# A decoder layer on one core: an early conditioning load moved up the load queue, one chunk's matmuls put in passes, and one weight split moved into the last softmax

## The chip, the core and the metric

The kernel runs on one core of one Trainium2 chip. The metric is the device time of one execution in microseconds (us): 1576.35 us is the median of three runs of the kernel before. Engines are named as in the profile: PE is TensorE's matmul row and PEld its weight-load row, DVE is VectorE, ACT is ScalarE, POOL is GpSimd, SP is SyncE, whose queue (SPq) issues nearly all loads. Instructions of one engine run in the order in which they are written; an instruction that has to wait holds back all that stand behind it on its engine.

## The reference

One layer of a decoder trunk over 512 tokens of width 2048, in float32, cut to what the change touches:

```python
c_act = jax.nn.silu(c)
mod = c_act @ w_ada[l] + b_ada[l]                  # 2048 -> 3 * 2048
shift, scale, gate = jnp.split(mod, 3, axis=-1)
h = rmsnorm(x, attn_norm_g[l]) * (1.0 + scale[:, None]) + shift[:, None]
proj = h @ w_in[l]                                 # q_lat, kv_lat, k_rope, z, u, v, z, g, g
...
p = jax.nn.softmax(s, axis=-1)                     # 16 heads, causal
...
merged = jax.nn.sigmoid(g_mla) * y_mla + jax.nn.sigmoid(g_sgu) * y_sgu
x = x + gate[:, None] * (merged @ w_out[l])
return rmsnorm(x, final_norm_g)
```

## The kernel before

**Products.** Every float32 operand of a large product is split in two: a rounded high part (ACT, a cast) and the remainder (DVE, a subtraction). A product is then three matmuls that add up in one PSUM bank: high by high, high by low, low by high. The helper `mm3` (lines 147 to 149) issues these three one behind the other. One matmul takes a 128x128 block of weights and a 128x512 moving operand.

**Weights as a stream.** The weights come in granules of up to 1024 columns, in one fixed order. `Stream` keeps that order: `dma_to(i)` issues loads up to granule `i` into three raw buffers (`wraw0` to `wraw2`), and `split_to(i)` splits granules up to `i` into two pairs of buffers (`w0h`/`w0l`, `w1h`/`w1l`): the cast is line 117, the subtraction line 118. A granule that is already split is not split again, for the loop begins at the first one that is not:

```python
    def split_to(self, i):
        i = min(i, len(self.src) - 1)
        while self.n_split <= i:
            ...
            self.nc.scalar.copy(hi[:, :n], raw[:, :n])
            self.nc.vector.tensor_tensor(out=lo[:, :n], in0=raw[:, :n], in1=hi[:, :n].bitcast(F32), op=ALU.subtract)
```

`get(i, ahead)` splits up to granule `i + ahead`, then issues loads three granules further. `load_before(granule, f)` hangs another load in front of a granule's own load on the same queue.

**The first stage.** The layer's input is multiplied chunk by chunk: 16 chunks of 128 input channels, each with the x tile `xt[j]` (256 KB, the `X` tiles), the first-stage granule `g1[j]` (512 KB, `wraw<-in_w`) and the adaLN scale chunk `KC + j` (KC is 16; 1 MB, `wada<-in_wada`). `ada_load` (line 356) loads an adaLN chunk and `ada_dot` reduces it on DVE against `silu(c)` (line 138, `wada<-wada,cact`). From that comes `gxA` (line 144), the factor of this chunk's 128 channels; ACT scales the x tile to the high part `hh[j]` (line 425), DVE makes the low part `hl[j]` (line 138). Eight banks `ps1[0]` to `ps1[7]` gather 1024 output columns, so that a chunk is 24 matmuls. For the first chunk they run pass by pass (line 434): all eight banks with the high parts, then all eight with the weights' low part, then all eight with `hl`. For the others they run bank by bank through `mm3`.

The order on DVE within a chunk is: dot, `gxA`, low part of the granule, `hl`, and the sum of squares of the chunk before (line 135, `cosT<-cosT,XS`). On ACT it is: cast of the granule, `hh`, square of the x tile. The four `wada` buffers first hold the small tiles from which `silu(c)` is spread over the partitions (`crow`, `csplit`, `pick`) and chunk 16; chunk 17 takes the buffer of `crow`, chunk 18 that of `csplit`, and so on, each once the old tile is free.

**The end of attention.** Heads 0 to 15 run one after the other: scores, softmax, projections of the next head, transposes of the softmax, product with v, gates. In `softmax` DVE masks and takes maxima, ACT exponentiates the four row blocks in two pairs (line 1559), and between the pairs a caller's function may run (`between`, which splits a granule). DVE then divides by the sums (lines 1547 and 142). The last head (15) has no next head; in the place of its projections stand the first two granules of the output projection, `go[0, 0]` and `go[0, 1]` (two times 24 matmuls over four banks), by `out_granule`. Behind them come the transposes of head 15's softmax (line 1577).

For head 15 the function that runs between the two pairs is `split_to(go[0, 0])`. That granule is next in the stream behind the last key granule, and `kproj(15)`, by `get` with one granule ahead, has split it by then.

Of the kernel before, what the change touches and what calls it, by code (L numbers as in the profile page):

```python
# [23 lines left out]
KC = D // P  # L24
NB = S // P
H = 16
# [101 lines left out]
def trunk_layer(ctx, tc, xT, xn, c, vecs, pos, wada, w1, w2, wv, wv3, wv4, wh, wh15, wq, wqr, wk, wvv, wo, wsT, bsp, gfin, out,  # L128
                dbg=None):
    nc = tc.nc  # L130
    ACT, DVE, PE, DMA = nc.scalar, nc.vector, nc.tensor, nc.sync
    LEFT, RIGHT = "left", "right"

    def tt(out, in0, in1, op):
        DVE.tensor_tensor(out=out, in0=in0, in1=in1, op=op)  # L135

    def stt(out, in0, scalar, in1, op0, op1, **kw):
        DVE.scalar_tensor_tensor(out=out, in0=in0, scalar=scalar, in1=in1, op0=op0, op1=op1, **kw)  # L138

    def ts(out, in0, s1, s2, op0, op1=None):  # L140
        if op1 is None:
            DVE.tensor_scalar(out=out, in0=in0, scalar1=s1, scalar2=None, op0=op0)
        else:
            DVE.tensor_scalar(out=out, in0=in0, scalar1=s1, scalar2=s2, op0=op0, op1=op1)

    def mm3(ps, ah, al, bh, bl, start, stop):
        PE.matmul(ps, ah, bh, start=start, stop=False)  # L147
        PE.matmul(ps, ah, bl, start=False, stop=False)  # L148
        PE.matmul(ps, al, bh, start=False, stop=stop)  # L149
# [18 lines left out]
    def nt(p, shape, dt, tag, **kw):  # L168
        uid[0] += 1
        return p.tile(shape, dt, tag=tag, name=f"{tag}_{uid[0]}", **kw)  # L170
# [11 lines left out]
    ws = Stream(nc, [(wp, f"wraw{i}") for i in range(3)], [(wp, f"w{i}") for i in range(2)])  # L182
# [79 lines left out]
    g1 = [ws.add(w1[k], GW) for k in range(KC)]  # L262
    z14 = lambda k, n: wh[H - 2, 0, k // 8][:, k % 8 * P:(k % 8 + n) * P]
    g2 = [ws.add([(0, S, w2[k][:, :S]), (S, P, z14(k, 1))], 640) for k in range(KC)]
    gq, gr, gk, gvv = {}, {}, {}, {}
# [35 lines left out]
    go = {}  # L301
# [9 lines left out]
    def get(i, ahead=1, run=1):  # L311
        r = ws.get(i, ahead)
        fs, pend[:] = pend[:run], pend[run:]
        for f in fs:
            f()
        return r
# [11 lines left out]
    def bank():  # L328
        n_bank[0] += 1
        return bank_at(ring[(n_bank[0] - 1) % len(ring)])  # L330
# [28 lines left out]
    def ada_dot(j):  # L359
        t = ada_tiles.pop(j)  # L360
        if j == KC:
            for q, sl in enumerate(quarters):
                stt(t[:, sl], t[:, sl], 1.0, cps[q], ALU.mult, ALU.mult, accum_out=dot0[:, q:q + 1])
            DVE.tensor_reduce(out=dots[:, j:j + 1], in_=dot0, axis=AX.X, op=ALU.add)
            ts(b1, vec[:, C_BADA + KC:C_BADA + 2 * KC], 1.0, None, ALU.add)
        else:
            stt(t, t, 1.0, cact, ALU.mult, ALU.mult, accum_out=dots[:, j:j + 1])

    def load_before(granule, f, *a):
        ws.before.setdefault(granule, []).append(lambda: f(*a))  # L370
# [3 lines left out]
    DMA.dma_start(vec, vecs)  # L374
    for j in range(KC):
        if j > 0:
            load_before(g1[max(j, 2)], ada_load, KC + j)
            load_before(g1[j], lambda j: DMA.dma_start(xt[j], xT[j]), j)
        load_before(SHIFT_AT[j], ada_load, j)
    load_before(g2[0], lambda: DMA.dma_start(cact_d, cact[0:1]))  # L380

    hh, hl = [None] * KC, [None] * KC
    ssx = cosT

    def square_of(j):
        if j == 0:
            ACT.activation(ssx, xt[j], AF.Square)
            return None
        sq = sqw[:, j % 2]
        ACT.activation(sq, xt[j], AF.Square)  # L390
        return sq
# [23 lines left out]
    ps1 = [bank() for _ in range(8)]  # L415
    sq = None
    for j in range(KC):
        if j > 0:
            ada_dot(KC + j)
        A = gxA[:, j:j + 1]  # L420
        ts(A, dots[:, KC + j:KC + j + 1], b1[:, j:j + 1], vec[:, C_GX + j:C_GX + j + 1], ALU.add, ALU.mult)
        wH, wL = get(g1[j], ahead=0)
        hh[j] = nt(hp.p, [P, S], F32R, f"hh{j}")
        hl[j] = nt(hp.p, [P, S], F32R, f"hl{j}")
        ACT.activation(hh[j], xt[j], AF.Copy, scale=A)  # L425
        stt(hl[j], xt[j], A, hh[j].bitcast(F32), ALU.mult, ALU.subtract)
        if sq is not None:
            tt(ssx, ssx, sq, ALU.add)
        sq = square_of(j)
        cols = [slice(m * P, (m + 1) * P) for m in range(8)]  # L430
        if j == 0:
            for a, b in ((wH, hh[j]), (wL, hh[j]), (wH, hl[j])):
                for m in range(8):
                    PE.matmul(ps1[m], a[:, cols[m]], b, start=(a is wH and b is hh[j]), stop=False)
        else:
            for m in range(8):
                mm3(ps1[m], wH[:, cols[m]], wL[:, cols[m]], hh[j], hl[j], False, j == KC - 1)
# [57 lines left out]
    for j in range(KC):  # L495
        fix_begin(j)
        wH, wL = get(g2[j])
# [136 lines left out]
    for st in range(KC):  # L634
# [5 lines left out]
        wH, wL = get(gb[st], ahead=0 if st == KC - 1 else 1)  # L640
# [63 lines left out]
    def place(s, us, f, *a):  # L704

        def full(s):
            own, (a, b) = busy.get(s, 0.0) + us, (busy.get(s + d, 0.0) for d in (-1, 1))
            return own > 3.3 or own + max(a, b) > 5.75

        while full(s):  # L710
            s += 1
        spend(s, us)
        on(s, BACK, f, *a)
        return s
# [240 lines left out]
    for g in range(H):  # L955
# [3 lines left out]
        a = s_ + 4  # L959
        on(a, BACK, sgu_scale)  # L960
        a = place(a, 0.29, sgu_weights)
        a = place(a, 0.29, sgu_weights_split)
        if g + 1 < H:
            on(a + 1, LOAD, sgu_load, g + 1)
        a = place(max(a, s_ + 5), 0.69, sgu_gain)
        a = place(a + 1, 0.69, sgu_split)
# [369 lines left out]
    for b in range(len(BLOCKS)):  # L1336
        if b == 1:
            ring[:], n_bank[0] = [5, 6], 0
        for g, (p, i) in enumerate(V7):
# [17 lines left out]
            if i == 0 and p in (1, 5, 6):  # L1357
# [3 lines left out]
            wH, wL = (w.rearrange("p (k h w) -> p k h w" if BLOCKS[b][0] == "v" else "p (h k w) -> p k h w", h=4, k=2)  # L1361
                      for w in vparts.pop((b, g)))
# [108 lines left out]
    def rproj(p):  # L1471
        wH, wL = get(gr[p])
        ps = bank_at(0)
        for k in range(6):
            sl = slice(k * P, (k + 1) * P)
            mm3(ps, wH[:, sl], wL[:, sl], lh[k], ll[k], k == 0, k == 5)
        return ps
# [47 lines left out]
    def scores(h):  # L1525
        qh, ql = qt.pop(h)
        kh, kl = kt.pop(h)
        q2 = qs.pop(h)
        s3, s2, s1 = bank(), bank(), bank()
        dst = {3: s3, 2: s2[:, :384], 1: s1[:, :256], 0: s1[:, 256:384]}  # L1530
        for i in (3, 2, 1, 0):
            ps = dst[i]
            n = (i + 1) * P
            q = slice(i * P, (i + 1) * P)
            mm3(ps, qh[:, q], ql[:, q], kh[:, :n], kl[:, :n], True, False)

            PE.matmul(ps, q2[:, q], krh[:, :n], start=False, stop=False)  # L1537
            PE.matmul(ps, q2[:, q], krl[:, :n], start=False, stop=True)  # L1538
        return dst
# [78 lines left out]
    def merge(n=None):  # L1618
        fs, merging[:] = merging[:n], merging[n:] if n else []
        for f in fs:  # L1620
            f()
# [22 lines left out]
    for h in range(H):  # L1644
        if h == H - 1:
            ring[:], n_bank[0] = [4, 5, 6, 7], 0
        dst = scores(h)
        more, odd = h + 1 < H, h % 2 == 1
        pair = h // 2 + 1
        first = go[0, 0] if not more else gr[pair] if not odd and 2 * pair < H else None  # L1650
        pr_, shares_ = softmax(h, dst, (lambda: ws.split_to(first)) if first is not None else None)
        if more:
            qproj(h + 1, lambda: merge(1 if h == H - 2 else None))
            if not odd and 2 * pair < H:
                rps = rproj(pair)
        else:
            pso = [bank_at(k) for k in range(NB)]
            for i in range(2):
                out_granule(0, i, pso)
        pa, fa = transposes(pr_, (0,))  # L1660
        fa()
        if h < GATED:
            for n in range(NB):
                g_ = gt[h][:, n * P:(n + 1) * P]
                ACT.activation(g_, g_, AF.Copy, scale=shares_[:, n:n + 1])
        pb, fb = transposes(pr_, (1,))
        fb()
        pc, fc = transposes(pr_, (2, 3))
        fc()
        if more:  # L1670
            kps = kproj(h + 1)
            kfinish(h + 1, kps)
        else:
            merge()
            pieces_at(h)
            DVE.tensor_reduce(out=dots[:, 2 * KC:2 * KC + NG], in_=partial, axis=AX.X, op=ALU.add)
            gate_sum(0, NG)
            out_granule(0, 2, pso)
            gate_turn(0, NG, bank(), nt(tp, [P, S], F32, "sig", bufs=3))()
        gate_ = gt[h]  # L1680
        if h < GATED:
            gate_ = nt(tp, [P, S], F32, "sig", bufs=3)
            ACT.copy(gate_, turn(gt[h]))
        tps = turn(vt[h])
        ops = pv(h, {**pa, **pb, **pc})
        merge_a(h, ops, tps, gate_)
        if not odd:
            pieces_at(h)
        if not odd and 2 * pair < H:
            m2 = at("m2", F32)  # L1690
            swapped(m2, rps)
        if more and odd:
            rfinish(pair, rps, m2)
            vproj(pair)
# [92 lines left out]
    for n in range(NB):  # L1787
        tk = slice(n * P, (n + 1) * P)

        for part, (o, w) in enumerate(((0, S),) if n < NB - 1 else ((0, half), (half, half))):  # L1790
            last = o + w == S
            ps = bank()[:, :w]
            for j in range(H):
                sl = slice((j % 2) * 512 + o, (j % 2) * 512 + o + w)
                wH, wL = wl[j // 2]
# [91 lines left out]
```

## Time and profile before

| what | us |
|---|---|
| three runs | 1574.80, 1576.35, 1576.39 |
| median of the three | 1576.35 |
| the profiled execution, its own time | 1576.21 |
| its span, from the first to the last instruction | 1574.5 |
| PE busy within the span | 1558.1 |
| DVE busy | 1221.5 |
| ACT busy | 801.4 |
| mean granted TensorE clock | 0.997 |

The page gives for each engine its busy time; the timeline gives single instructions with their start, their length and, in brackets, how long the engine sat idle before and what released it; the view by windows gives for a stretch of time each engine's busy time with the number of instructions, the granted clock (1.00 is full) and what the DMA engines moved. All times are counted from the span's start. Matmuls overlap in the records: the distance from one start to the next is what a matmul costs, and it is shorter than the length shown.

### The profile page before, as it was taken

How to read it: one execution, taken by the hardware profiler on the slowest of the kernel's cores; microseconds unless marked ns; L12 is line 12 of the kernel's file. 1: busy time of each engine (PE TensorE's matmuls, PEld its weight loads, DVE VectorE, ACT ScalarE, POOL GpSimd, SP SyncE). 2: the span in 40 equal slices, each digit the busy share in tenths (PEclk: the TensorE clock that was granted, in tenths of full speed). 3: DMA queues.
4: the chain of work that ended last, by engine and by line, in shares of the span. 5: the costliest groups of instructions: out<-in, count | busy, mean ns of one | idle time of the engine just before them, and what ended most of it. 6: DMA issues, size and time to landing. Idle time of an engine off the chain costs nothing. (4 is left out here: it accounts for less than half of the span.)

```text
span 1574.5 us, 20617 instructions
## 1 busy us (share of the span) xinstructions
PE 1558.1 (99%) x7400; PEld 1297.6 (82%) x7400; DVE 1221.5 (78%) x1665; ACT 801.4 (51%) x1238; POOL 70.3 (4%) x67
## 2 busy tenths in 40 slices
PE   9999999999999999999999999999999999999998
PEld 7888778888888888888888888887888888888886
DVE  7989777778787879787879697968777777865753
ACT  4344555546554546455546464647655566532332
POOL 0000000100010000010100010100000000000000
PEclk9999999999999999999999999999999999999999
DMA  9979565859786877787767785966433333338722
GB/s 380 357 265 341 180 182 169 237 140 266 232 231 173 230 210 213 208 220 202 206 169 205 207 246 157 261 172 211 148 118 119 127 116 117 98 127 331 263 88 107
DMA packets 237224, 316.16 MB, mean 201 GB/s; under 512 B 16201, under 2 KB 184193, under 8 KB 231489
## 3 DMA queue, kind: packets, MB, share of 16 engines
q1 hardware_dynamic: 214066, 291.25, 55.9%
q0 software_dynamic: 22912, 23.07, 9.6%
q8 instruction: 58, 0.95, 0.3%
q10 hardware_dynamic: 144, 0.52, 0.1%
q14 instruction: 44, 0.36, 0.1%
HBM read 291.11 MB, written 23.68 MB: 200 GB/s over the span
## 5 line engine op out<-in xcount | busy, mean ns | idle before, releaser
L135 DVE TENSOR_TENSOR X<-X,X 128x1024 fp32r<-128x1024 f32 (+2 forms) x110 | 129.4, 1182 | 29.7 <-ACT X L620 26.8
L620 ACT CAST w0h<-X 128x1024 fp32r<-128x1024 f32 x70 | 73.6, 1052 | 95.0 <-PE ps L1369 56.5
L620 ACT CAST X<-X 128x1024 fp32r<-128x1024 f32 x69 | 72.5, 1051 | 89.8 <-PE ps L1369 52.4
L620 ACT CAST w1h<-X 128x1024 fp32r<-128x1024 f32 x70 | 73.6, 1051 | 82.5 <-PE ps L1369 44.4
L135 DVE TENSOR_TENSOR w0l<-X,w0h 128x1024 fp32r<-128x1024 f32 x70 | 85.6, 1222 | 27.1 <-ACT w0h L620 26.8
L135 DVE TENSOR_TENSOR w1l<-X,w1h 128x1024 fp32r<-128x1024 f32 x70 | 85.5, 1222 | 26.0 <-ACT w1h L620 24.3
L147 PE MATMUL ps<-hh,w1h 128*128 128x512 f32 (+1 forms) x260 | 103.9, 400 | 1.6 <-ACT hh L425 1.4
L148 PE MATMUL ps<-hl,w1h 128*128 128x512 f32 (+1 forms) x260 | 102.3, 393 | 0.5 <-DVE hl L138 0.5
L149 PE MATMUL ps<-hh,w1l 128*128 128x512 f32 (+1 forms) x260 | 102.2, 393 | 0.0
L118 DVE TENSOR_TENSOR w0l<-wraw,w0h 128x1024 fp32r<-128x1024 f32 (+4 forms) x61 | 64.3, 1053 | 42.0 <-ACT w0h L117 40.3
L135 DVE TENSOR_TENSOR X<-wraw,X 128x1024 f32<-128x1024 f32 (+1 forms) x66 | 80.6, 1221 | 19.5 <-ACT X L620 17.0
L117 ACT CAST w0h<-wraw 128x1024 fp32r<-128x1024 f32 (+4 forms) x61 | 56.0, 918 | 75.0 <-issue 22.0
L1370 PE MATMUL ps<-w1l,hh 128*128 128x512 f32 x236 | 92.3, 391 | 1.7 <-DVE w1l L135 1.7
L147 PE MATMUL ps<-hh,w0h 128*128 128x512 f32 x238 | 93.7, 394 | 0.0
L117 ACT CAST w1h<-wraw 128x1024 fp32r<-128x1024 f32 (+4 forms) x60 | 50.5, 841 | 83.2 <-issue 23.9
L148 PE MATMUL ps<-hl,w0h 128*128 128x512 f32 x238 | 92.8, 390 | 0.0
L149 PE MATMUL ps<-hh,w0l 128*128 128x512 f32 x238 | 92.7, 389 | 0.0
L1370 PE MATMUL ps<-w0l,hh 128*128 128x512 f32 x236 | 92.2, 391 | 0.4 <-DVE w0l L135 0.4
L1368 PE MATMUL ps<-w1h,hh 128*128 128x512 f32 x236 | 92.0, 390 | 0.2 <-ACT w0h L620 0.2
L1368 PE MATMUL ps<-w0h,hh 128*128 128x512 f32 x236 | 92.0, 390 | 0.0
L1369 PE MATMUL ps<-w1h,hl 128*128 128x512 f32 x236 | 91.9, 389 | 0.0
L1369 PE MATMUL ps<-w0h,hl 128*128 128x512 f32 x236 | 91.9, 389 | 0.0
(398 smaller groups left out, 4380.9 us busy)
## 6 DMA issues: line engine op xcount, KB each, us to landing
X<-in_wh SPq DMA_DIRECT2D x131, 512.0 KB, 4.9
wada<-in_wada SPq DMA_DIRECT2D x39, 1024.0 KB, 7.0
wraw<-in_wo SPq DMA_DIRECT2D x32, 512.0 KB, 4.4
wraw<-in_wh SPq DMA_DIRECT2D x21, 512.0 KB, 5.4
wraw<-in_wh POOLq DMA_DIRECT2D x21, 512.0 KB, 7.7
X<-in_wv SPq DMA_DIRECT2D x17, 512.0 KB, 3.5
X<-in_wh SPq DMA_DIRECT2D x22, 384.0 KB, 3.5
half<-in_w SPq DMA_DIRECT2D x32, 256.0 KB, 4.3
```

The source lines that it names most:

```text
L117: self.nc.scalar.copy(hi[:, :n], raw[:, :n])
L118: self.nc.vector.tensor_tensor(out=lo[:, :n], in0=raw[:, :n], in1=hi[:, :n].bitcast(F32), op=ALU.subtract)
L135: DVE.tensor_tensor(out=out, in0=in0, in1=in1, op=op)
L147: PE.matmul(ps, ah, bh, start=start, stop=False)
L148: PE.matmul(ps, ah, bl, start=False, stop=False)
L149: PE.matmul(ps, al, bh, start=False, stop=stop)
L620: ACT.copy(hi, t)
L1368: PE.matmul(ps[t].rearrange("p (h w) -> p h w", h=4), xh[:, tk], wH[:, k], start=st, stop=False, skip_group_check=True)
L1369: PE.matmul(ps[t].rearrange("p (h w) -> p h w", h=4), xl[:, tk], wH[:, k], start=False, stop=False, skip_group_check=True)
L1370: PE.matmul(ps[t].rearrange("p (h w) -> p h w", h=4), xh[:, tk], wL[:, k], start=False, stop=sp, skip_group_check=True)
```

## The change

```diff
     DMA.dma_start(vec, vecs)
     for j in range(KC):
         if j > 0:
-            load_before(g1[max(j, 2)], ada_load, KC + j)
+            load_before(g1[j], ada_load, KC + j)
             load_before(g1[j], lambda j: DMA.dma_start(xt[j], xT[j]), j)
         load_before(SHIFT_AT[j], ada_load, j)
...
-        if j == 0:
+        if j <= 1:
             for a, b in ((wH, hh[j]), (wL, hh[j]), (wH, hl[j])):
                 for m in range(8):
-                    PE.matmul(ps1[m], a[:, cols[m]], b, start=(a is wH and b is hh[j]), stop=False)
+                    PE.matmul(ps1[m], a[:, cols[m]], b, start=(j == 0 and a is wH and b is hh[j]), stop=False)
         else:
             for m in range(8):
                 mm3(ps1[m], wH[:, cols[m]], wL[:, cols[m]], hh[j], hl[j], False, j == KC - 1)
...
     for h in range(H):
         if h == H - 1:
             ring[:], n_bank[0] = [4, 5, 6, 7], 0
+            ws.split_to(go[0, 0])
         dst = scores(h)
         more, odd = h + 1 < H, h % 2 == 1
         pair = h // 2 + 1
-        first = go[0, 0] if not more else gr[pair] if not odd and 2 * pair < H else None
+        first = go[0, 1] if not more else gr[pair] if not odd and 2 * pair < H else None
         pr_, shares_ = softmax(h, dst, (lambda: ws.split_to(first)) if first is not None else None)
```

No instruction is added or taken away on any engine: PE, DVE, ACT, POOL and SP have as many as before. The order moves at three places.

On SP, at the program's start, in the order of issue (`wada_194` is adaLN chunk 17 after the change, `wada_197` the same chunk before; `wada_199` is chunk 18; `X_35` is the tile that holds x chunks 0 and 1, `wraw_1` granule `g1[1]`):

```order
 L374 DMA vec_88<-in_vecs 128x92
+L356 DMA wada_194<-in_wada 128x2048
 L378 DMA X_35_179<-in_xT 128x512
-L98 DMA wraw_1_195<-in_w 128x1024
-L356 DMA wada_197<-in_wada 128x2048
+L98 DMA wraw_1_197<-in_w 128x1024
 L356 DMA wada_199<-in_wada 128x2048
 L378 DMA X_36_180<-in_xT 128x512
```

Chunk 17 stood behind x chunk 1 and granule 1, and now stands ahead of both; chunk 18 and all that follows keep their places.

On PE, in the first stage's second chunk (`hh_65` and `hl_66` are `hh[1]` and `hl[1]`, `w1h_367` and `w1l_368` the two parts of granule 1, `ps_53` to `ps_60` the eight banks), before:

```order
L434 MATMUL ps_60_325<-hl_63_337,w0h_327 128x512
L147 MATMUL ps_53_318<-hh_65_376,w1h_367 128x512
L148 MATMUL ps_53_318<-hl_66_377,w1h_367 128x512
L149 MATMUL ps_53_318<-hh_65_376,w1l_368 128x512
L147 MATMUL ps_54_319<-hh_65_376,w1h_367 128x512
L148 MATMUL ps_54_319<-hl_66_377,w1h_367 128x512
```

and after, at the end of the first of its three passes:

```order
L434 MATMUL ps_58_323<-hh_65_376,w1h_367 128x512
L434 MATMUL ps_59_324<-hh_65_376,w1h_367 128x512
L434 MATMUL ps_60_325<-hh_65_376,w1h_367 128x512
L434 MATMUL ps_53_318<-hh_65_376,w1l_368 128x512
L434 MATMUL ps_54_319<-hh_65_376,w1l_368 128x512
```

The 24 matmuls are the same; `hl[1]` was read by the second of them and is now read by the seventeenth, `w1l` by the third and now by the ninth.

On DVE, in the softmax of head 15 (`d_1395` and `hl_1833` hold its exponentials, `mx` its maxima and sums, `wraw_97` is granule `go[0, 1]`, `wraw_98` granule `go[0, 2]`):

```order
 L142 TENSOR_SCALAR d_1395_9078<-d_1395_9078,mx_12144 128x512
 L142 TENSOR_SCALAR d_1395_9078<-d_1395_9078,mx_12144 128x384
+L118 TENSOR_TENSOR w0l_12162<-wraw_97_11920,w0h_12161 128x1024
 L1547 RECIPROCAL mx_12144<-mx_12144 128x2
 L142 TENSOR_SCALAR hl_1833_12145<-hl_1833_12145,mx_12144 128x256
 L142 TENSOR_SCALAR hl_1833_12145<-hl_1833_12145,mx_12144 128x128
-L118 TENSOR_TENSOR w0l_12171<-wraw_97_11920,w0h_12170 128x1024
 L118 TENSOR_TENSOR w1l_12201<-wraw_98_12021,w1h_12200 128x1024
```

and on ACT at the same place:

```order
 L1559 ACTIVATE d_1395_9078,mx_12144<-ps_1829_12121,mx_12144 128x512
 L1559 ACTIVATE d_1395_9078,mx_12144<-ps_1830_12122,mx_12144 128x384
+L117 CAST w0h_12161<-wraw_97_11920 128x1024
 L1559 ACTIVATE hl_1833_12145,mx_12144<-ps_1831_12123,mx_12144 128x256
 L1559 ACTIVATE hl_1833_12145,mx_12144<-ps_1831_12123,mx_12144 128x128
-L117 CAST w0h_12170<-wraw_97_11920 128x1024
 L117 CAST w1h_12200<-wraw_98_12021 128x1024
```

The granule that moves is `go[0, 1]`, the output projection's second: both halves of its split stood behind the softmax and now stand between its two pairs. The new call `ws.split_to(go[0, 0])` ahead of the scores issues nothing, since that granule is split already.

## The prediction

> **What bounds the kernel now.** I read the page's busy times first, then the waits of PE, then the two places of the change in the timeline. PE is busy for nearly the whole span, and the view of waits (time in all, times, longest) shows the few stretches in which it is held up:
>
> ```profile
> PE 1558.1 (99%) x7400; PEld 1297.6 (82%) x7400; DVE 1221.5 (78%) x1665; ACT 801.4 (51%) x1238; POOL 70.3 (4%) x67
> PE ps L147 <- ACT hh L425: 1.4, 1, 1.4
> PE ps L148 <- DVE w0l L118: 0.8, 1, 0.8
> PE ps L148 <- DVE hl L138: 0.5, 1, 0.5
> ```
>
> So a microsecond counts only where PE waits or runs slowly, and these three waits lie at the change's places. The view by windows adds what the waits don't show (columns: length; PE, PEld, DVE, ACT and POOL busy; granted clock, DMA share, GB/s):
>
> ```profile
> 11.08:16.90 5.82, 5.73 (x24) 4.42 (x24) 3.15 (x3) 1.41 (x2) 0.48 (x1) 1.00 1.02 412
> 16.90:18.20 1.30, 0.01 (x1) 0.01 (x1) 1.26 (x4) 0.78 (x2) 0.00 (x0) 1.00 1.04 429
> 20.10:23.50 3.40, 3.40 (x10) 2.65 (x9) 3.36 (x6) 1.35 (x3) 0.00 (x0) 0.52 1.03 418
> 80.00:100.00 20.00, 20.00 (x90) 16.57 (x89) 16.66 (x21) 9.26 (x14) 0.00 (x0) 1.00 0.65 210
> ```
>
> PE is idle from 16.90 to 18.20, and from 20.10 to 23.50 it is busy at about half the clock. At 80 to 100 the DMA engines have slack (a share of 0.65).
>
> **The first stage: what the second chunk loses.** PE's starts:
>
> ```profile
> 13.02 1.98 PE L434 MATMUL ps<-hh,w0l 128*128 128x512 f32 x8
> 14.84 1.97 PE L434 MATMUL ps<-hl,w0h 128*128 128x512 f32 x8
> 18.19 0.49 PE L147 MATMUL ps<-hh,w1h 128*128 128x512 f32 x1 [1.38 <-ACT hh L425]
> 19.23 0.50 PE L148 MATMUL ps<-hl,w1h 128*128 128x512 f32 x1 [0.55 <-DVE hl L138]
> 26.18 0.39 PE L147 MATMUL ps<-hh,w0h 128*128 128x512 f32 x1
> ```
>
> Eight matmuls take 14.84 - 13.02 = 1.82, or 0.2275 each. Chunk 0 thus leaves PE free at 14.84 + 1.82 = 16.66; chunk 2 starts at 26.18. Between lie 9.52 us for 24 matmuls that need 24 x 0.2275 = 5.46. The 4.06 lost are 1.53 before the first (18.19 - 16.66), 0.81 before the second (19.23 - 18.19 - 0.23), and the remaining 1.72 in the half-clock stretch. It follows at once on two gaps of 2.34 in all within some 3 us, and I take these for its cause.
>
> The Trainium skill, "TensorE: Matmul & The Clock Gate", section "Part 1: The HAM clock gate (the "warmup" mystery)", gives half clock as the state after an idle window of about 3.4 us, in windows that run free of the kernel's start. The trace disagrees on the condition (no gap here is that long) and agrees on the length (3.40 in the row above); by the page's length the stretch costs 3.4 / 2 = 1.7, by the rows 1.72. By its free-running windows the stretch would be missing in some executions: the lowest run shown, 1574.80, lies 1.55 under the median.
>
> What held the second chunk up, on DVE and ACT:
>
> ```profile
> 11.32 0.78 DVE L138 SCALAR_TENSOR_TENSOR hl<-X,gxA,hh 128x512 fp32r<-128x512 f32 x1
> 11.45 1.04 ACT L117 CAST w1h<-wraw 128x1024 fp32r<-128x1024 f32 x1
> 14.77 2.29 DVE L138 SCALAR_TENSOR_TENSOR wada<-wada,cact 128x2048 f32<-128x2048 f32 x1 [2.67 <-DMA wada<-in_wada]
> 17.11 0.27 DVE L144 TENSOR_SCALAR gxA<-dots,b,vec 128x1 f32<-128x1 f32 x1
> 17.30 1.22 DVE L118 TENSOR_TENSOR w1l<-wraw,w1h 128x1024 fp32r<-128x1024 f32 x1
> 17.42 0.72 ACT L425 ACTIVATE hh<-X,gxA 128x512 fp32r<-128x512 f32 x1 [4.93 <-DVE gxA L144]
> 18.43 0.75 DVE L138 SCALAR_TENSOR_TENSOR hl<-X,gxA,hh 128x512 fp32r<-128x512 f32 x1
> 19.09 2.28 DVE L138 SCALAR_TENSOR_TENSOR wada<-wada,cact 128x2048 f32<-128x2048 f32 x1
> 19.16 1.05 ACT L117 CAST w0h<-wraw 128x1024 fp32r<-128x1024 f32 x1 [0.50 <-DMA wraw<-in_w]
> ```
>
> Chunk 17 lands at 14.77, the last of three transfers: x chunk 1 (256 KB), granule 1 (512 KB), chunk 17 (1 MB). Behind it everything is a chain on DVE, and the early granule only waits.
>
> **Loads reordered.** No bytes are added, the DMA engines run at 412 GB/s throughout, so the three land together by 14.77 as before, in another order. Chunk 17 now has 768 KB behind it: 0.786 MB / 412 GB/s = 1.91, an estimate from the windows row, so it lands at 12.86. Its dot starts there (DVE is free from 12.10); `gxA` ends 17.11 + 0.27 - 14.77 = 2.61 later, at 15.47. Granule 1 is now last, at 14.77, and its cast stands ahead of `hh` on ACT: 14.79 to 15.83, then `hh` from 15.87. The first matmul followed `hh`'s start by 18.19 - 17.42 = 0.77: 16.64, against 16.66 when PE is free. The first wait goes to about nothing. It is now granule 1 that sets it: each microsecond that it lands later is one that PE waits.
>
> The load that moves is issued from SP, and behind it wait x chunk 1, granule 1 and all later loads:
>
> ```profile
> 3.20 1.08 SPq L378 DMA_DIRECT2D X<-in_xT  x1
> 4.32 0.47 SPq L98 DMA_DIRECT2D wraw<-in_w  x1
> 5.08 2.97 SPq L356 DMA_DIRECT2D wada<-in_wada  x2
> 7.07 0.69 DVE L138 SCALAR_TENSOR_TENSOR wada<-wada,ps 128x512 f32<-128x512 f32 x1 [2.02 <-DMA wada<-in_wada]
> ```
>
> It has to wait until 5.08 for its buffer, now with two loads behind it that were out at 3.20 and 4.32; they go out at about 5.4 and 5.9. At 5.08 only part of chunk 16 has landed (its first half at 7.07), with its second half, x chunk 0 and the vectors still queued, so the engines have work meanwhile. I cost this at nothing; without that cover it would cost what they stand idle.
>
> **Passes.** `w1l` is made at 15.87 to 17.09, and PE first needs it eight matmuls in, at 18.48; `hl` follows 1.13 after the start of `w1l` (18.43 - 17.30), 17.00 to 17.75, needed at 20.30. Both are hidden, where bank by bank PE would need `hl` at 16.89 and wait some 0.9. With neither gap I expect no half-clock stretch. Chunk 1 ends at 16.66 + 5.46 = 22.12.
>
> **What is late next.** Chunk 2 must be ready 4 us earlier. Its dot follows `hl` by 19.09 - 18.43 = 0.66, at 17.66 (its load came behind chunk 17: 14.77 + 1.048 MB / 412 GB/s = 17.3, in time); `gxA` is ready at 20.27. Granule 2 lands at 19.1 as before (its cast waited on DMA), cast to 20.21, `hh` from 20.30, first matmul possible at 21.07: in time for 22.12. `w0l` starts 20.25 and `hl` ends at 20.25 + 1.13 + 0.75 = 22.13; PE needs it at 22.35. This is the tightest margin, 0.2. After it the margins grow, as the steady cycle on DVE shows:
>
> ```profile
> 35.13 2.29 DVE L138 SCALAR_TENSOR_TENSOR wada<-wada,cact 128x2048 f32<-128x2048 f32 x1
> 38.17 1.22 DVE L118 TENSOR_TENSOR w1l<-wraw,w1h 128x1024 fp32r<-128x1024 f32 x1 [0.43 <-ACT w1h L117]
> 40.58 2.29 DVE L138 SCALAR_TENSOR_TENSOR wada<-wada,cact 128x2048 f32<-128x2048 f32 x1
> ```
>
> A chunk takes DVE 40.58 - 35.13 - 0.43 = 5.02 and the DMA engines 1.835 MB / 413 GB/s = 4.44, PE 5.46. PE's lead therefore holds, and the term is the whole 4.06. Its bounds: no more than 4.06, since nothing else is lost there; no less than 0.8, if only the passes' wait goes.
>
> **The last head.** Here PE stops for the low part of `go[0, 1]`:
>
> ```profile
> 1388.93 0.20 ACT L1559 ACTIVATION_READ_ACCUMULATOR d<-ps,mx 128x1 f32 x1
> 1389.38 0.82 DVE L142 TENSOR_SCALAR d<-d,mx 128x512 f32<-128x512 f32 x2
> 1390.03 0.20 ACT L1559 ACTIVATION_READ_ACCUMULATOR hl<-ps,mx 128x1 f32 x1
> 1390.12 1.04 ACT L117 CAST w0h<-wraw 128x1024 fp32r<-128x1024 f32 x1
> 1390.46 0.55 DVE L142 TENSOR_SCALAR hl<-hl,mx 128x256 f32<-128x256 f32 x2
> 1391.19 1.23 DVE L118 TENSOR_TENSOR w0l<-wraw,w0h 128x1024 fp32r<-128x1024 f32 x1 [0.19 <-ACT w0h L117]
> 1391.21 0.50 PE L147 MATMUL ps<-w0h,b 128*128 128x512 f32 x1
> 1392.47 0.50 PE L148 MATMUL ps<-w0l,b 128*128 128x512 f32 x1 [0.76 <-DVE w0l L118]
> 1392.82 0.40 PE L149 MATMUL ps<-w0h,g 128*128 128x512 f32 x1
> 1397.87 0.38 PE L1577 MATMUL ps<-ident,hl 128*128 128x128 f32 x2
> ```
>
> The third matmul starts at 1392.82 where 1391.21 + 0.46 = 1391.67 was possible: 1.15 lost. The cast moves ahead of the second pair of exponentials, which end at 1390.23, and follows the first pair, which ends at 1389.13: it ends at 1389.13 + 1.04 = 1390.17. The raw granule is there, since its buffer's load went out before head 15. DVE is done with the first pair's division at 1390.20, and `w0l` ends at 1391.43 instead of 1392.42: 1.0 gained, 0.15 left. Bounds: 0 if the cast can't start earlier, 1.15 to 1.3 if no wait is left. The price is that the second pair's division ends at about 1392.2 instead of 1391.0; the transposes that read it start at 1397.87, so over 4 us of cover hide it. The line ahead of the scores issues nothing and costs nothing.
>
> **Sum.** 1576.21 (the profiled execution; its span of 1574.5 and 1.7 around it) - 4.06 - 1.0 = 1571.15. The median lies 0.14 above that execution; I take **1571.2**. What is gained early reaches the end if nothing later is tied to the transfers' own pace: with a share of 0.65 at 80 to 100 there is 7 us of slack in those 20, more than the 4 that PE comes earlier, and the view of waits has none for PE from 23.5 to 102. I count all of it.
>
> **Rivals.**
> *PE outruns its data* (less gain): chunk 2 or 3 waits 1 to 2 us for `hl` or a granule. For it speaks the margin of 0.2 and a row of estimates behind it; against it the cycles of 5.02 and 4.44. 1572.2 to 1573.2.
> *The transfers share the engines*, so that chunk 17 still lands near 14.77: the reordering doesn't do what it says. Then PE starts at 18.19 again, only the passes' 0.81 and the last head's 1.0 are won: 1574.4, or 1572.7 if the half clock goes too. Against it, granule 1 was in place for its cast at 11.45 with no DMA wait, over 3 us before chunk 17 behind it. In the Trainium skill, "DMA: Bandwidth & Descriptors", section "Queues, rings and completion order" says that completion is not in order per issuing engine; the rows just named agree rather with order.
> *The last head gains nothing*: 1572.2. Its waits are all on rows shown, so I give it little.
> *Slower: PE stutters.* PE starts chunk 1 early, then stops in each of chunks 2 to 5 for `hl` or a granule long enough (about as at 16.66 to 19.23, some 2 us) to bring a half-clock stretch of 1.72 each time. Data then set the pace, the 4.06 are given back, and four new stretches instead of one cost 3 x 1.72 = 5.2: 1576.2 - 1.0 + 5.2 = 1580.4. It decides from two such stops on (1576.9); DVE's 5.02 a chunk against PE's 5.46 speaks against even a second.
>
> **How the numbers follow.** Forecast 0.68 (own range 1570.3 to 1572.2), outrun 0.13, shared transfers 0.10, no gain in the last head 0.05, stutter 0.04. A measurement of this kernel can tell 0.2%, or 3.15 us: faster means under 1573.2. That is all of the forecast, of the outrun and of the last head's case, and a fifth of the shared transfers, 0.88, less a little for the second's upper end: 0.87. Same takes the rest of these, 0.09; slower the stutter, 0.04. The range is 1569.8 to 1573.9: below, 1.4 for a full end of the last wait and small waits that fall otherwise; above, the outrun and half of the shared transfers.
>
> **What would show it.** Right: the second chunk's first matmul (then line 434) at 16.6 to 16.8 with no wait on `hh`, no window at 0.5 clock between 16 and 27, chunk 2's first matmul near 22.1; the dot of chunk 17 before 13; in head 15, matmuls of `go[0, 1]` with at most 0.2 of wait. Wrong: a DMA wait on the cast of `w1h` beyond 15, waits on line 138 or 118 in chunks 2 to 4, a half clock that only moves.

## The result, and the profile after

| | before, us | after, us |
|---|---|---|
| median of ten runs | 1575.76 (1574.64 to 1576.78) | 1571.53 (1570.85 to 1573.59) |
| profiled execution | 1576.21 | 1571.03 |
| its span | 1574.5 | 1569.3 |
| first matmul of chunks 1, 2, 3 of the first stage | 18.19, 26.18, 31.62 | 16.39, 21.97, 27.59 |
| first matmul of `go[0, 0]`, transposes of head 15 | 1385.53, 1397.87 | 1381.49, 1392.73 |

The ratio of the times is 0.9974, with a 95% interval of 0.9965 to 0.9984: 0.26% faster. The forecast was 1571.2, the range 1569.8 to 1573.9. The two profiled executions differ by 5.18 us, the medians by 4.23; the forecast's terms came to 5.06. One of the ten executions after the change took 1573.59, the others 1571.80 at most; no run here explains that one.

The busy times on the page of the changed kernel show PE shorter by 3.4, though it has as many instructions as before:

```profile
PE 1554.7 (99%) x7400; PEld 1295.6 (83%) x7400; DVE 1220.7 (78%) x1665; ACT 802.0 (51%) x1238; POOL 69.5 (4%) x67
PE ps L1370 <- DVE w1l L135: 1.7, 4, 0.5
PE ps L434 <- ACT hh L425: 1.5, 1, 1.5
```

The other two rows are the head of the view of PE's waits (time in all, times, longest). The three waits that bounded the kernel before are gone from it. The one on `hh` that is left is chunk 0's, at 10.77, before any product can start (it was 0.7 before, next to another wait of 1.1 that both kernels have); line 1370 runs from 220 to 1079 us, far from the change, and its waits were there before. What was PE's idle and half-clock time in the second chunk shows in the view by windows of the changed kernel (columns as before):

```profile
16.90:18.20 1.30, 1.30 (x7) 1.04 (x7) 1.30 (x3) 0.00 (x0) 0.00 (x0) 1.00 1.04 433
20.10:23.50 3.40, 3.40 (x16) 2.58 (x16) 3.29 (x5) 1.33 (x3) 0.00 (x0) 1.00 1.03 422
```

PE was busy for 0.01 of the first stretch, now for all of it. In the second the clock was 0.52, now it is 1.00, and 16 matmuls start where 10 did. The timeline of the changed kernel, for the first stage:

```profile
11.67 2.29 DVE L138 SCALAR_TENSOR_TENSOR wada<-wada,cact 128x2048 f32<-128x2048 f32 x1
14.53 1.97 PE L434 MATMUL ps<-hl,w0h 128*128 128x512 f32 x8
14.66 1.05 ACT L117 CAST w1h<-wraw 128x1024 fp32r<-128x1024 f32 x1 [3.43 <-DMA wraw<-in_w]
15.62 0.72 ACT L425 ACTIVATE hh<-X,gxA 128x512 fp32r<-128x512 f32 x1
16.39 2.11 PE L434 MATMUL ps<-hh,w1h 128*128 128x512 f32 x8
16.89 0.74 DVE L138 SCALAR_TENSOR_TENSOR hl<-X,gxA,hh 128x512 fp32r<-128x512 f32 x1
20.15 1.98 PE L434 MATMUL ps<-hl,w1h 128*128 128x512 f32 x8
21.40 0.75 DVE L138 SCALAR_TENSOR_TENSOR hl<-X,gxA,hh 128x512 fp32r<-128x512 f32 x1
21.97 0.39 PE L147 MATMUL ps<-hh,w0h 128*128 128x512 f32 x1
22.20 0.19 PEld L148 LDWEIGHTS ps<-hl,w0h 128*128 128x128 f32 x1 [0.27 <-DVE hl L138]
22.20 0.50 PE L148 MATMUL ps<-hl,w0h 128*128 128x512 f32 x1
22.55 0.40 PE L149 MATMUL ps<-hh,w0l 128*128 128x512 f32 x1
```

Chunk 17's dot no longer waits for a transfer; the DMA wait now stands at the cast of granule 1, and this cast, with `hh` behind it, sets the earliest start of chunk 1. It is just in time, as forecast: chunk 0 is through at 14.53 + 1.82 = 16.35, and chunk 1 starts at 16.39. `hl` of chunk 1 ends at 17.63, and PE needs it at 20.15. The one place where something is late is chunk 2's `hl`, which ends at 22.15: the view of waits has nothing there, but the weight load of the matmul that reads it (PEld, 22.20) was held 0.27, and the next matmul follows at 0.35 instead of 0.23. And in head 15, the timeline of the changed kernel:

```profile
1384.98 1.04 ACT L117 CAST w0h<-wraw 128x1024 fp32r<-128x1024 f32 x1
1385.92 0.48 ACT L1559 ACTIVATE hl<-ps,mx 128x256 f32<-128x256 f32 x1
1386.06 1.22 DVE L118 TENSOR_TENSOR w0l<-wraw,w0h 128x1024 fp32r<-128x1024 f32 x1
1387.02 0.39 PE L147 MATMUL ps<-w0h,b 128*128 128x512 f32 x1
1387.34 0.50 PE L148 MATMUL ps<-w0l,b 128*128 128x512 f32 x1
1387.39 0.55 DVE L142 TENSOR_SCALAR hl<-hl,mx 128x256 f32<-128x256 f32 x2
1387.68 0.40 PE L149 MATMUL ps<-w0h,g 128*128 128x512 f32 x1
1392.73 0.38 PE L1577 MATMUL ps<-ident,hl 128*128 128x128 f32 x2
```

The cast runs ahead of the second pair of exponentials, `w0l` is ready at 1387.28, and the third matmul follows the first by 0.66, where it was 1.61; at the full pace it would be 0.46.

### The profile page after: what moved, and what is told of

Same layout as the page of the kernel before. It is cut to its first block, busy times and chain, and to the rows that moved or that the text cites. A ratio compares the mean times of both kernels' runs of the same rounds, so it can differ in the third digit from the quotient of the medians.

```text
span 1569.3 us, 20618 instructions
## 1 busy us (share of the span) xinstructions
PE 1554.7 (99%) x7400; PEld 1295.6 (83%) x7400; DVE 1220.7 (78%) x1665; ACT 802.0 (51%) x1238; POOL 69.5 (4%) x67
## 5 line engine op out<-in xcount | busy, mean ns | idle before, releaser
L147 PE MATMUL ps<-hh,w1h 128*128 128x512 f32 x252 | 100.1, 397 | 0.3 <-ACT w1h L117 0.3
L149 PE MATMUL ps<-hh,w1l 128*128 128x512 f32 x252 | 98.4, 390 | 0.0
L148 PE MATMUL ps<-hl,w1h 128*128 128x512 f32 x252 | 98.4, 390 | 0.0
L135 DVE TENSOR_TENSOR X<-wraw,X 128x1024 f32<-128x1024 f32 (+1 forms) x66 | 80.6, 1221 | 19.5 <-ACT X L620 17.0
```

## The experiments

All of them in one table, by their profiled executions. The second column is the time from chunk 0's first matmul to chunk 2's, so that a later or earlier start of the whole doesn't count; 48 matmuls at 0.2275 would take 10.92. The third runs from the first matmul of `go[0, 0]` to head 15's transposes. The ratios come from the comparison with runs of the kernel before on the same chip (their medians were 1576.12 beside the first four experiments, 1575.17 beside the next three, 1575.98 beside the last) and differ a little from the quotients of these medians.

| kernel | chunk 0 to chunk 2 | last head | profiled, us | median, us | ratio to before, with interval |
|---|---|---|---|---|---|
| before | 15.10 | 12.34 | 1576.21 | 1575.76 | 1 |
| before, again | 15.47 | 12.29 | 1576.18 | 1575.57 | 0.9998 (0.9989 to 1.0007) |
| loads alone | 11.60 | 12.31 | 1573.12 | 1573.12 | 0.9984 (0.9975 to 0.9993) |
| passes alone | 12.70 | 12.31 | 1573.72 | 1573.91 | 0.9987 (0.9978 to 0.9996) |
| last head alone | 13.89 | 11.19 | 1573.73 | 1574.32 | 0.9992 (0.9983 to 1.0001) |
| before, gaps filled | 13.81 | 12.28 | 1574.98 | 1575.67 | 0.9999 (0.9990 to 1.0008) |
| after, chunk 18 early too | 13.41 | 11.21 | 1573.35 | 1574.41 | 0.9994 (0.9985 to 1.0003) |
| after, weights behind the conditioning | 11.88 | 11.20 | 1571.34 | 1571.23 | 0.9974 (0.9963 to 0.9985) |
| after | 11.20 | 11.24 | 1571.03 | 1571.53 | 0.9974 (0.9965 to 0.9984) |
| after, again | 11.36 | 11.20 | 1570.72 | 1571.24 | 0.9971 (0.9961 to 0.9982) |

The theory behind them is that of the prediction: two waits in chunk 1 bring a stretch at half clock, the loads' order takes away the first wait, the passes the second, and the last head is worth 1.0 by itself.

**Before, again.** No edit; it asks whether the half-clock stretch belongs to the kernel.

> The kernel before, unchanged, once more. Theory: the half-clock stretch of 3.4 us behind the second chunk's gaps comes in some executions and not in others, since the times of before spread over 1574.6 to 1576.8. Then this profile has either a half-clock stretch near 20 us and an own time of about 1576, or none and about 1574.6 (1.7 us less); the second chunk's first matmul comes 1.3 to 1.6 us after PE is free in both. Rival: the stretch belongs to the order of the work and comes every time; then this profile has it again, and the spread of the times has another cause.

Its stretch, by windows (granted clock is the third number from the end):

```profile
16.04:19.46 3.42, 1.15 (x5) 0.41 (x3) 3.38 (x6) 1.27 (x3) 0.00 (x0) 1.00 1.01 414
19.50:22.85 3.35, 3.35 (x8) 2.66 (x9) 3.31 (x4) 1.96 (x3) 0.00 (x0) 0.50 1.05 423
22.95:24.00 1.05, 1.05 (x6) 0.87 (x5) 1.05 (x3) 0.17 (x1) 0.00 (x0) 1.00 0.94 378
```

The stretch came again, as long as before. By itself this doesn't tell a fixed property from one that comes often. The mean granted clock of its eleven executions says more: six have 0.997 (median 1576.45), four have 0.999 (1574.75) and one 0.998. The next kernels show what the difference is.

**The three parts, each alone.** The loads:

```diff
-            load_before(g1[max(j, 2)], ada_load, KC + j)
+            load_before(g1[j], ada_load, KC + j)
```

> Only the order of the loads is changed; the second chunk still runs bank by bank, and the last head is as before. Theory: hh of chunk 1 is in time, so its first matmul comes at 16.4 to 16.7 with no wait, but its second waits some 0.9 us for hl; one gap of 0.9 brings no half clock. Chunk 2 starts at 22.9 to 23.1, 3.1 to 3.3 earlier than in the profile of before; time 1573.0 (1576.2 - 4.06 + 0.9). Rival (loads alone carry it, the passes are for nothing): chunk 2 starts at 22.0 to 22.2, time 1572.2. Rival (any gap brings the half clock): chunk 2 starts at 24.7, time 1574.7.

Its timeline:

```profile
15.14 1.98 PE L434 MATMUL ps<-hl,w0h 128*128 128x512 f32 x8
16.95 0.39 PE L147 MATMUL ps<-hh,w1h 128*128 128x512 f32 x1
17.63 0.50 PE L148 MATMUL ps<-hl,w1h 128*128 128x512 f32 x1 [0.29 <-DVE hl L138]
22.98 0.39 PE L147 MATMUL ps<-hh,w0h 128*128 128x512 f32 x1
```

Chunk 1 starts as soon as chunk 0 is through (15.14 + 1.82 = 16.96), so the wait of 1.5 goes with the loads' order alone. The second matmul still comes 0.68 behind the first, 0.45 too late, for `hl`; 0.9 was expected. From chunk 0 to chunk 2 the kernel is 3.50 shorter, not 3.1 to 3.3.

The passes:

```diff
-        if j == 0:
+        if j <= 1:
...
-                    PE.matmul(ps1[m], a[:, cols[m]], b, start=(a is wH and b is hh[j]), stop=False)
+                    PE.matmul(ps1[m], a[:, cols[m]], b, start=(j == 0 and a is wH and b is hh[j]), stop=False)
```

> Only the second chunk's matmuls are put in passes; loads and last head are as before. Theory: its first matmul still waits for hh and comes 1.3 to 1.6 after PE is free; the 0.8 wait for hl is gone. If the one gap of 1.5 still brings a half-clock stretch, chunk 2 starts at 25.3 and the time is 1575.4; if not, at 23.6 and 1573.7. Rival (the passes alone carry it): chunk 2 near 22.1, time 1572.2.

Its timeline, and its view by windows:

```profile
18.18 2.11 PE L434 MATMUL ps<-hh,w1h 128*128 128x512 f32 x8 [1.35 <-ACT hh L425]
23.75 0.39 PE L147 MATMUL ps<-hh,w0h 128*128 128x512 f32 x1
```

```profile
19.40:22.90 3.50, 3.50 (x17) 2.87 (x16) 3.46 (x5) 2.11 (x3) 0.00 (x0) 1.00 1.04 421
```

The first wait stays, the second is gone, and so is the half clock: chunk 1 takes 23.75 - 18.18 = 5.57. One wait of this length brought no stretch in this execution, and none of the eleven has a mean clock under 0.998.

The last head:

```diff
-        first = go[0, 0] if not more else gr[pair] if not odd and 2 * pair < H else None
+        first = go[0, 1] if not more else gr[pair] if not odd and 2 * pair < H else None
```

> Only the split of go[0, 1] is moved between the last head's two pairs of exponentials; the first stage is as before. Theory: the wait for the low part falls from about 1.2 to 0.2, so 1.0 to 1.1 less between the first matmul of granule go[0, 0] and the transposes: time 1575.1 with a half-clock stretch in the first stage, 1573.5 without. Rival (the second pair's delay eats it): transposes come no earlier, time as before.

The last head became 1.15 shorter (12.34 to 11.19), much as in the changed kernel (1.10). The surprise stands in its first stage, which is that of the kernel before to the last instruction, in the timeline and by windows:

```profile
18.54 0.50 PE L147 MATMUL ps<-hh,w1h 128*128 128x512 f32 x1 [1.78 <-ACT hh L425]
19.57 0.50 PE L148 MATMUL ps<-hl,w1h 128*128 128x512 f32 x1 [0.54 <-DVE hl L138]
24.91 0.39 PE L147 MATMUL ps<-hh,w0h 128*128 128x512 f32 x1
```

```profile
19.40:22.90 3.50, 3.33 (x15) 2.77 (x16) 3.46 (x5) 1.88 (x3) 0.00 (x0) 1.00 1.04 418
```

Both waits are there, the first longer than before, the second as long, but no half clock. Chunk 1 takes 24.91 - 18.54 = 6.37, against 26.18 - 18.19 = 7.99 in the profile of before. The stretch is thus worth 1.6, and it comes in some executions of the same instructions and not in others: of this kernel's eleven, three have a mean clock of 0.997.

The loads alone take 3.50 off, the passes alone 2.40 (chunk 0 to chunk 2), and the last head 1.15; together the first two take 3.90, not 5.90. They don't add up, since either takes the stretch away (none of their 22 executions has a mean clock of 0.997, against 16 of the 33 of before beside them), and the loads also shorten the second wait, from 0.81 to 0.45.

**Is it the idle time that brings the half clock?** The kernel before, with the two gaps filled by matmuls on a tile of zeros, and the causal mask's fill moved behind the first stage, since the tile of zeros is the mask's own, not yet filled:

```diff
...
+            if j == 1:
+                for _ in range(24):
+                    PE.matmul(ps1[0][:, :P], zero, zero, start=False, stop=False)
+                PE.matmul(ps1[0], wH[:, cols[0]], hh[j], start=False, stop=False)
+                for _ in range(12):
+                    PE.matmul(ps1[0][:, :P], zero, zero, start=False, stop=False)
+                PE.matmul(ps1[0], wH[:, cols[0]], hl[j], start=False, stop=False)
+                PE.matmul(ps1[0], wL[:, cols[0]], hh[j], start=False, stop=False)
-            for m in range(8):
+            for m in range(1 if j == 1 else 0, 8):
...
```

> The kernel before, with 24 small matmuls of a zero tile (128 columns, added to the open bank of output columns 0 to 127, so that nothing changes in it) ahead of the second chunk's first matmul and 12 ahead of its second: PE is busy in the two gaps, and no data come earlier. The fill of the causal mask is moved behind the first stage. Theory (the gaps bring the half clock): no half-clock stretch between 16 and 27 us in the profile and in no execution; the second chunk's first two matmuls as late as before, chunk 2 at 24.4 to 24.6, and the times lose their upper group: all within 0.6 us of about 1574.7. Rival (the stretch has another cause): times spread over 2 us as those of before.

Its timeline and windows:

```profile
16.59 1.51 PE L436 MATMUL ps<-mask 128*128 128x128 bf16 x24
18.35 0.50 PE L437 MATMUL ps<-hh,w1h 128*128 128x512 f32 x1 [0.25 <-ACT hh L423]
24.78 0.39 PE L147 MATMUL ps<-hh,w0h 128*128 128x512 f32 x1
```

```profile
19.40:22.90 3.50, 3.50 (x18) 2.88 (x16) 3.46 (x4) 2.05 (x3) 2.08 (x1) 1.00 1.04 421
```

No stretch in this profile, and a mean granted clock of 0.998 or 0.999 in all eleven executions, where eight of the 23 of the kernel before that ran on the same chip had 0.997. But the expectation's other half failed: its times still spread from 1573.69 to 1576.84, and their median is that of before. So the clock is not the only thing that moves the time of this kernel from one execution to the next; the other source stayed open.

**Does the time follow the load order?** On the changed kernel, chunk 18 (1 MB) is put ahead of granule 1 too:

```diff
-            load_before(g1[j], ada_load, KC + j)
+            if j != 2:
+                load_before(g1[j], ada_load, KC + j)
+            if j == 1:
+                load_before(g1[j], ada_load, KC + 2)
```

> The changed kernel, with adaLN chunk 18 also queued ahead of x chunk 1 and granule 1: 1 MB more stands ahead of granule 1. Theory (granule 1's landing now sets the second chunk's start): it lands 2.5 us later, at 17.1; the cast ends at 18.2 and the first matmul comes at 19.0, 2.4 to 2.6 after PE is free. That gap brings a half-clock stretch in most executions: chunk 2 starts at 24.5, or 26.2 with the stretch; time 1573.5 or 1575.2. Rival (the conditioning chunks set the pace, weights are in time anyway): no wait, time 1571.2 or less.

Its timeline:

```profile
14.88 1.98 PE L437 MATMUL ps<-hl,w0h 128*128 128x512 f32 x8
17.21 1.04 ACT L117 CAST w1h<-wraw 128x1024 fp32r<-128x1024 f32 x1 [5.63 <-DMA wraw<-in_w]
18.93 2.12 PE L437 MATMUL ps<-hh,w1h 128*128 128x512 f32 x8 [2.08 <-ACT hh L428]
24.53 0.40 PE L147 MATMUL ps<-hh,w0h 128*128 128x512 f32 x1
```

The cast comes 17.21 - 14.66 = 2.55 later than in the changed kernel, and chunk 1 follows it by 2.54. One more transfer of 1.048 MB ahead, at the 419 GB/s of its windows, is 2.50. So the granule's cast does follow what is queued ahead of it, and PE follows the cast. Of its eleven executions, five have a clock of 0.997, at 1574.41 to 1575.84, and five one of 0.999, at 1573.35 to 1573.88: with a wait of 2.1 the half clock comes in about half of them again, if the clock is read as its mark. Most of them had been expected to have it. The profiled one, at 0.999, has no stretch.

**Can more be had?** The first chunk, too, waits for conditioning. On the changed kernel, the vectors and chunk 16 are put ahead of granule 0 (now on SP's queue instead of ACT's) and x chunk 0, and x chunk 1 behind granule 1:

```diff
-    ws.dma_to(0)
...
+    DMA.dma_start(vec, vecs)
...
+    ws.first = DMA
+    ws.dma_to(0)
...
-    DMA.dma_start(vec, vecs)
...
-            load_before(g1[j], lambda j: DMA.dma_start(xt[j], xT[j]), j)
+            load_before(g1[j + 1 if j == 1 else j], lambda j: DMA.dma_start(xt[j], xT[j]), j)
```

> The changed kernel, with the loads in the order in which they are waited for: c, the vectors, adaLN chunk 16, granule 0 (now on SP, no longer beside it on ACT's queue), x chunk 0, chunk 17, granule 1, x chunk 1. Theory (the start is bound by what has to be moved before it): chunk 16 lands about 1.2 earlier, hh of chunk 0 comes 0.3 to 0.9 earlier, and granule 1 lands 0.6 earlier, ahead of x chunk 1; the second chunk follows without a wait of more than 0.3. Gain 0.3 to 0.6 in the first stage, time 1570.7 to 1571.2. Rival (DVE or ACT sets chunk 0, or later chunks give it back): chunk 3's first matmul comes no earlier than 27.4, time 1571.5.

Its timeline:

```profile
10.57 2.11 PE L435 MATMUL ps<-hh,w0h 128*128 128x512 f32 x8 [1.31 <-ACT hh L426]
13.45 2.29 DVE L138 SCALAR_TENSOR_TENSOR wada<-wada,cact 128x2048 f32<-128x2048 f32 x1 [1.64 <-DMA wada<-in_wada]
16.10 0.72 ACT L426 ACTIVATE hh<-X,gxA 128x512 fp32r<-128x512 f32 x1 [0.47 <-DVE gxA L144]
16.88 2.11 PE L435 MATMUL ps<-hh,w1h 128*128 128x512 f32 x8 [0.57 <-ACT hh L426]
```

No gain: chunk 0 starts 0.2 earlier at most, and gives it back in chunk 1, where chunk 17's dot again waits for its transfer, until 13.45. The median is level with the changed kernel's, and chunk 3 starts at 28.14, as the rival said (no earlier than 27.4). What sets the start of chunk 0 stays open.

**The changed kernel, again,** to see whether its gain holds in a second sample.

> The changed kernel, unchanged, once more, beside the kernel before on one chip. Theory (no gap is left that can bring the half clock, wherever its window falls): no half-clock stretch between 12 and 27 us in this profile either, the second chunk's first matmul within 0.1 of PE being free, chunk 2 at 21.9 to 22.3; times within 1 us of 1571.4, where those of before spread over 3 us. Gain over the median of before 4.0 to 5.0. Rival (the first profile was a lucky one): a stretch or a wait over 0.5 in the second chunk, times that spread as those of before.

It does: 1571.24 (eight runs, 1570.47 to 1571.71) against 1575.98 (1574.40 to 1577.70). Its windows and timeline:

```profile
19.40:22.90 3.50, 3.50 (x17) 2.72 (x16) 3.37 (x6) 2.27 (x3) 0.00 (x0) 1.00 1.04 417
```

```profile
14.71 1.97 PE L434 MATMUL ps<-hl,w0h 128*128 128x512 f32 x8
16.74 2.11 PE L434 MATMUL ps<-hh,w1h 128*128 128x512 f32 x8
22.32 0.39 PE L147 MATMUL ps<-hh,w0h 128*128 128x512 f32 x1
```

No half clock again, and no execution of this sample at a clock of 0.997. Chunk 1 starts 0.21 behind the end of chunk 0 (14.71 + 1.82 = 16.53), for here the cast of granule 1 came at 15.02; 0.1 was expected, and chunk 2 comes at 22.32, just past the expected 22.3.

## Why the prediction was right

**The bound.** PE's waits and its half-clock stretch were the right place to look. The three waits went, and nothing took their place beyond some tenths of a microsecond at the start of chunk 1 and in chunks 1 and 2.

**The loads.** The mechanism held: chunk 17 lands earlier, the cast of granule 1 takes over as what sets chunk 1 (14.66, forecast 14.79), `hh` starts at 15.62 (15.87), the first matmul at 16.39 (16.64). One estimate was off without consequence: chunk 17's dot was put at 12.86 and ran at 11.67. So at least 2.99 us lie between its landing and the cast of granule 1, where 1.91 were estimated for the 768 KB. The step that failed there is that the three land strictly one behind the other: in these 2.99 us the DMA engines moved 421 GB/s, or 1.26 MB, and only 0.786 MB of it can be x chunk 1 and granule 1, so loads issued behind them were moving too. The dot isn't what PE waits for, and the sum didn't feel it. The cost of nothing for the reordered queue on SP held as well, since granule 1 landed at 14.66, where the last of the three had landed at 14.77 (in the second profile of the changed kernel its cast came at 15.02).

**The passes.** As forecast, `w1l` and `hl` are both covered. By the kernel with the loads alone, what they add to the loads is only the second wait's rest, 6.03 - 5.58 = 0.45 from chunk 1 to chunk 2, half of the 0.9 that the prediction put on it; the stretch goes with either part.

**What is late next.** Chunk 2's `hl` was named as the tightest margin. It was put at 0.2 and measured as none: 0.12 is lost there. After it, DVE's cycle is shorter than PE's as computed, and the waits of PE from 12 to 30 us are empty.

**The sum.** Chunk 3 starts 31.62 - 27.59 = 4.03 earlier, against a term of 4.06. Of that, 0.31 is chunk 0's own start (10.77 against 11.08), which ranged from 10.77 to 11.38 over the kernels that load for chunk 0 in the same order, and which I don't put down to the change. From chunk 0's first matmul on the gain is 3.72; that the term came out within 0.03 is luck. The 0.34 missing are 0.04 before chunk 1, 0.12 in chunk 1 (21.97 - 16.39 = 5.58, where 24 matmuls at 0.2275 would be 5.46; with the passes alone it took 5.57), and 0.18 in chunk 2 (27.59 - 21.97 = 5.62, against 31.62 - 26.18 = 5.44), of which the late `hl` is 0.12. The last head brought 12.34 - 11.24 = 1.10, against 1.0. All 4.03 + 1.10 = 5.13 are still there at the last matmul, which starts at 1561.25 instead of 1566.39, 5.14 earlier: what is gained early reached the end, as the slack of the transfers said it would.

**The one step that was only half true** is the sum's starting point. I took the profiled execution of before, half-clock stretch and all, to stand for the median. The kernels above show the stretch in some executions and not in others. Of the 33 runs of before beside the first four experiments, 16 have a mean clock of 0.997, like both profiled executions with a stretch, and a median of 1576.3; five have 0.999 and a median of 1574.62. So of the term of 4.06, some 1.6 are won only in those executions of before that have the stretch, 16 or more of the 33. This is one reason why the medians differ by less than the profiles (5.18), by 4.23 and, in the second sample, by 4.74. It isn't the whole of it: the profile of before lies 0.45 above its median of ten, but that of the changed kernel lies 0.50 below its own, and the kernel with the filled gaps has a spread that the clock doesn't explain. The forecast started from a profile that it took to lie 0.14 below the median, by three runs; by ten it lies 0.45 above. That 1571.2 held all the same owes something to luck.

**The rivals.** PE outran its data by 0.12, once in each profile of the changed kernel (0.11 in the second). That shared transfers keep chunk 17 near 14.77 is refuted by the dot at 11.67 and by the loads alone, whose chunk 1 starts on time; that the transfers overlap somewhat is what the 421 GB/s above show. The last head's gain is there by itself. The stutter would have needed two stretches or more; between chunk 0 and PE's last matmul the changed kernel has none in two profiles, and it has no mean clock under 0.998 in 18 executions.

## What to carry to other kernels

Of several transfers that one piece of work needs, the one with the longest chain behind it goes first in the queue, and the bulky one whose chain is short can come last: with the bytes unchanged, this alone was worth 3 us here, with the half-clock stretch that went with it. Where the operands of a new chunk are made while the matmul engine already waits for them, all banks with the first operand before any with the next gives the others eight or sixteen matmuls of cover. Price a stretch at reduced clock apart from the waits beside it, and read more than one execution before counting it in full: the same waits brought it in some and not in others.

## What the hardware showed

The half clock doesn't follow from the length of the gaps alone. With the gaps counted from the end of chunk 0 as in the prediction, the profile of before has 1.53 and 0.81, and the stretch; before, again, has 1.90 and 0.80, and the stretch; the kernel with the last head alone, with the same instructions there, has 1.94 and 0.80, and none. Nor does it begin at a fixed distance from the gap. In the profile of before, by windows:

```profile
16.57:19.98 3.41, 1.48 (x6) 0.84 (x5) 3.37 (x6) 2.06 (x3) 0.00 (x0) 1.00 1.01 408
20.00:23.40 3.40, 3.40 (x9) 2.63 (x8) 3.36 (x5) 1.45 (x3) 0.00 (x0) 0.50 1.03 419
23.45:24.40 0.95, 0.95 (x6) 0.78 (x5) 0.95 (x3) 0.00 (x0) 0.00 (x0) 1.00 1.03 405
1569.53:1569.63 0.10, 0.00 (x0) 0.00 (x0) 0.10 (x2) 0.10 (x1) 0.00 (x0) 1.00 0.00 0
1569.64:1569.74 0.10, 0.00 (x0) 0.00 (x0) 0.10 (x1) 0.10 (x1) 0.00 (x0) 0.50 0.00 0
```

It starts at about 20.0, 0.8 behind the end of the second wait (19.23); when the kernel before ran again, at about 19.5, 0.1 behind it (19.37); it was 3.4 long both times. (The 3.40 in the row that the prediction shows is the length of the stretch of time asked for, and its clock of 0.52 says that it misses the edge; the rows here measure it.)

The last two rows show that the clock falls once more at the end, when PE is done (its last matmul starts at 1566.39). That happens in all ten profiles, and a rule can be worked out from it. From the rise to this last fall it is 1569.63 - 23.40 = 1546.2 in the profile of before and 1569.11 - 22.87 = 1546.2 when it ran again, 453 times 3.413 both times, although the two stretches lie 0.5 apart against the same matmuls. So the clock changes on a grid of 3.413 us, which can be counted back from the last fall in every profile. PE's idle time between two lines of the grid, from the view by windows (it counts an engine as busy to the end of a matmul, so it shows less than a gap counted from start to start):

| kernel | last fall of the clock | windows of the grid | PE idle in each | clock behind it |
|---|---|---|---|---|
| before | 1569.63 | 16.57 to 19.98 | 1.93 | 0.50 |
| before, again | 1569.11 | 16.04 to 19.46 | 2.27 | 0.50 |
| after, its last matmuls | 1563.71 | 1560.29 to 1563.71 | 2.18 | 0.50 |
| last head alone | 1567.83 | 14.77 to 18.18, to 21.59 | 1.43, 0.89 | 1.00 |
| passes alone | 1567.20 | 14.13 to 17.55, to 20.96 | 0.72, 0.63 | 1.00 |
| after, chunk 18 early too | 1567.63 | 14.56 to 17.98, to 21.39 | 1.13, 0.95 | 1.00 |
| the same, ahead of chunk 0 | 1567.63 | 7.74 to 11.15 | 1.89 | 1.00 |

In the ten profiles, from 7 us on, the clock was at half behind every such window with 1.93 us of idle time or more, and it fell behind none with 1.89 or less; the border is not sharper than that, since the ends of matmuls are modelled. The two gaps of before bring the stretch when enough of both falls into one window; a line of the grid that divides their idle time prevents it, as in the kernel with the last head alone. In the changed kernel the gaps behind chunk 0 come to some 0.3 in all, too little wherever the grid lies. The mean clock of an execution also holds the stretch at the end, of 3.6 to 5.6 us in these profiles; with such ends 0.997 means that the early stretch was there and 0.999 that it was not, and 0.998 leaves it open.

This grid fits the windows running free of the kernel's start of which the Trainium skill speaks, "TensorE: Matmul & The Clock Gate", section "Part 1: The HAM clock gate (the "warmup" mystery)". The runs don't agree with the page's condition of a whole idle window of about 3.4 us, for 1.93 idle of 3.41 was enough here.
